# Forming two kinds of elementwise results on GpSimd instead of VectorE around the start of w_down

## The chip, the cores and the metric

The kernel runs on one core of a Trainium2 chip. The metric is device time in microseconds for one execution. Five engines matter: TensorE (PE in the profile, its weight loads PEld), VectorE (DVE), ScalarE (ACT), GpSimd (POOL) and SyncE (SP), which here issues the DMAs. Each engine takes its instructions in the order in which they stand in its queue; a row that waits holds up what stands behind it.

## The reference

One encoder layer: two attention mixers, an output projection, then a gated feed-forward network with a depthwise convolution, and a final RMSNorm. SEQ = D_MODEL = 1024, D_FF = 2816, all float32. The change lies in the feed-forward part:

```python
h2 = rmsnorm(x, g_ffn[i]) * (1 + scale2) + shift2
u = depthwise_conv_seq(h2 @ w_up[i], conv_w[i], conv_b[i])       # three taps along the sequence
u_val, u_gate = jnp.split(u, 2, axis=-1)
x = x + gate2 * ((jax.nn.gelu(u_gate, approximate=True) * u_val) @ w_down[i])
return rmsnorm(x, g_final)
```

## The kernel before, in words

Every float32 product is made of a high and a low half of each operand (`h`, `l` at a tile's name): three matmuls (lines L948, L949, L950) take high by high, high by low, low by high. On top of that w_up and w_down go by Strassen's scheme in Winograd's form, with seven block products in place of eight. `STEPS` names their operands: 11 x B11, S2 x T2, S1 x T1, S3 x T3, 12 x B21, S4 x B22, 22 x T4. S1 to S4 are sums and differences of a weight's four blocks; T1 to T4 of the other matrix's: T1 = B12 - B11, T2 = B22 - T1, T3 = T2 - B11, T4 = B21 - T2.

**w_up** runs in 22 jobs, t = 0 to 21, of 84 matmuls each. What `products` yields goes to `done` and `finish`: ScalarE adds the bias (L1138), VectorE the convolution's taps (L1144), ScalarE takes the gelu of the gate half (L1170), then the product of the two halves is formed (L1171, 128x1024), and SP stores it to DRAM, `a_scr` (L1172, `as<-big`).

**w_down** runs in 12 jobs, `jobs = (g0, q)`: three groups of three rows each (g0 = 0, 3, 6; `G` is 3), and four jobs of 63 matmuls to a group. A job's weights come in two loads (`down_load`, L1055, tiles `wraw`, of which there are two), and `a_operands` makes of them S1 (L912), S2 (L913), S3 (L914) on GpSimd and S4 on VectorE (L921). `split` makes the halves: high on ScalarE (L55), low on GpSimd (L56): `whi`/`wlo` of blocks 11 and 12, `wsh`/`wsl` of S2 with S1 and of S3 with 22, and a `big` tile for S4. The last reader of a raw tile lets SP load the next job's.

A group's operands come from `b_operands`, once for four jobs; I call the place where the next group's are made a transition. The first lies at the end of w_up and serves jobs 0 to 3, the second serves jobs 4 to 7, the third jobs 8 to 11. SP reads the stored rows (L1007), GpSimd forms T1 (L1018) and T2 (L1019) for the group's three rows. `moved` then copies a source to PSUM on ScalarE (`stage`, L998), takes the high half on ScalarE (L999) and the low half on VectorE (L1000). Its `then` is called with the copy in PSUM: for T2 it forms T3 in the place of B11 (L1028), for B21 it forms T4 (L1030). Behind the 12 jobs four rows are left over for an end phase.

A planner orders the instructions of each engine by a model of their times where the code does not set the order by hand; in `finish` the last job of w_up gets a lower priority (`offset=-300`).

Of the kernel before, what the change touches and what calls it, by code (L numbers as in the profile page):

```python
# [12 lines left out]
OP = mybir.AluOpType  # L13
# [6 lines left out]
FF = 22  # L20
# [8 lines left out]
def hybrid_encoder(tc, xT, c, w_ada, small, w_in, p1_bias, p23_bias, na_bias, ln2_mult, ident, w_br, w_out,  # L29
                   w_up, w_down, out):  # L30
    nc = tc.nc
    act, dve, pool, pe, sp = nc.scalar, nc.vector, nc.gpsimd, nc.tensor, nc.sync
# [897 lines left out]
    def products(st, n, moving, done, seq=range(7), in_psum=False):  # L930

        p, c = {}, {}

        def bank(x_):
            p[x_] = ps.tile([128, 512], FT, name="pj", bufs=6)
            return p[x_]

        def tmp(x_):
            c[x_] = wide()
            return c[x_]  # L940
        for j in seq:
            a, b = STEPS[j]
            x_ = "abcdacd"[j]
            psum = bank(x_) if j < 4 else p[x_]
            whi, wlo = st[a]
            for k in range(n):
                bhi, blo = moving(b, k)
                pe.matmul(psum, whi[:, k], bhi, start=j < 4 and k == 0, stop=False, skip_group_check=True)  # L948
                pe.matmul(psum, whi[:, k], blo, start=False, stop=False, skip_group_check=True)  # L949
                pe.matmul(psum, wlo[:, k], bhi, start=False, stop=k == n - 1, skip_group_check=True)  # L950
                if k == 1:
                    yield -1
            if j == 0:
                act.activation(tmp("t"), psum, AF.Copy)
            elif j == 1:
                dve.tensor_tensor(c["t"], psum, c["t"], OP.add)
            elif j == 2:
                dve.tensor_tensor(tmp("v"), psum, c["t"], OP.add)
            elif j == 3:
                dst = p["b"] if in_psum else c["v"]  # L960
                dve.tensor_tensor(dst, psum, c["v"], OP.add)  # L961
                done(1, 1, dst)
            elif j == 4:
                done(0, 0, psum)
            elif j == 5:
                dve.tensor_tensor(psum, psum, c["t"], OP.add)
                done(0, 1, psum)
            else:
                dst = psum if in_psum else c["t"]
                dve.tensor_tensor(dst, psum, c["t"], OP.add)  # L970
                done(1, 0, dst)
            yield j
# [8 lines left out]
    def wide(dtype=FT):  # L981
        return keep.tile([128, 512], dtype, name="wc", bufs=5)

    def big(shape, dtype=FT):
        return keep.tile(shape, dtype, name="big", bufs=9)
# [7 lines left out]
    def moved(n, src, then=None):  # L993

        hi, lo = ((work2 if n in ("B11", "T2", "T1", "T3") else work1[n]).tile(
            [128, 512], FR, name=n + e, bufs=G) for e in "hl")
        copy = ps.tile([128, 512], FT, name="stage", tag=next(stages))
        act.activation(copy, src, AF.Copy)  # L998
        act.activation(hi, src, AF.Copy)  # L999
        dve.tensor_tensor(lo, copy, f(hi), OP.subtract)  # L1000
        if then:
            then(copy)
        return hi, lo

    def a_load(i):
        ra = big([128, S])
        sp.dma_start(ra, a_scr[i])  # L1007
        return ra

    def b_operands(g0, mov):  # L1010

        ra = [[a_load(i + 11 * j) for j in range(2)] for i in range(g0, g0 + G)]
        b = [(r[0][:, :512], r[0][:, 512:], r[1][:, :512], r[1][:, 512:]) for r in ra]
        yield
        t1 = [wide() for _ in range(G)]
        for k in range(G):
            b11, t2, b21, b22 = b[k]
            pool.tensor_tensor(t1[k], t2, b11, OP.subtract)  # L1018
            pool.tensor_tensor(t2, b22, t1[k], OP.subtract)  # L1019
        yield  # L1020
        for n, src in (("B11", 0), ("T2", 1), ("T1", None), ("T3", 0), ("B21", 2), ("B22", 3), ("T4", 2)):
            mov[n] = []
            for k in range(G):
                b11, t2, b21, b22 = b[k]

                def then(copy):
                    if n == "T2":
                        dve.tensor_tensor(b11, copy, b11, OP.subtract)  # L1028
                    if n == "B21":
                        dve.tensor_tensor(b21, copy, t2, OP.subtract)  # L1030
                mov[n].append(moved(n, t1[k] if n == "T1" else b[k][src], then))
            yield
# [103 lines left out]
    with tc.tile_pool(name="up", bufs=2, reuse_waits="tile") as work:  # L1136
        def conv_in(y, t, hf, src):
            act.activation(y[:, halves[hf]], src, AF.Identity, bias=conv[:, 3, t:t + 1], scale=conv[:, 1, t:t + 1])  # L1138

        def conv_taps(y, t, ph):  # L1140
            w0, w2 = conv[:, 0, t:t + 1], conv[:, 2, t:t + 1]

            def tap(dst, src, wt):
                dve.scalar_tensor_tensor(y[:, dst], src, wt, y[:, dst], OP.mult, OP.add)  # L1144
            tap(slice(256, 768), ph[0], w0)
            tap(slice(768, 1024), ph[1][:, 0:256], w0)
            tap(slice(1, 256), ph[1][:, 256:511], w0)
            tap(slice(0, 256), ph[0][:, 256:512], w2)
            tap(slice(256, 768), ph[1], w2)
            tap(slice(768, 1023), ph[0][:, 1:256], w2)  # L1150

        def up_products(t, st, seq=range(7)):
            u, ys = [{}, {}], {i: big([128, S]) for i in range(2) if t == FF - 1}

            def done(i, hf, src):
                u[i][hf] = src
                if len(u[i]) == 1 and t < 2:
                    return
                with tc.high_priority(offset=-300 if t == FF - 1 else 0):
                    finish(i, hf)  # L1160

            def finish(i, hf):
                if i not in ys:
                    ys[i] = big([128, S])
                for n in range(2) if t < 2 else (hf,):
                    conv_in(ys[i], t + FF * i, n, u[i][n])
                if len(u[i]) == 2:
                    conv_taps(ys[i], t + FF * i, u[i])
                if len(u[0]) + len(u[1]) == 4:
                    act.activation(ys[1], ys[1], AF.Gelu_apprx_tanh)  # L1170
                    dve.tensor_tensor(ys[0], ys[0], ys[1], OP.mult)  # L1171
                    sp.dma_start(a_scr[t], ys[0])  # L1172
            return products(st, 4, lambda n, k: late[n][k] if n in late else (ops[n][0][:, k], ops[n][1][:, k]), done,
                            seq)
# [25 lines left out]
        t2 = big([128, 2, 512])  # L1200
        t2 = [t2[:, 0], t2[:, 1], wide(), wide()]
# [256 lines left out]
```

## Time and profile before

| what | before |
|---|---|
| median of 3 runs | 1569.3 us (1565.9 to 1570.37) |
| the profiled execution | 1566.2 us, span of its trace 1564.4 us |
| granted TensorE clock, mean | 0.982 |
| TensorE busy | 1509.5 us, 96% of the span |
| VectorE busy | 1024.4 us, 65% |
| ScalarE busy | 805.8 us, 52% |
| GpSimd busy | 801.8 us, 51% |

The span runs from the first to the last instruction of the trace. In the timelines each row has its start, its duration (us), engine, line, operation, `out<-in`, shape and count, and in brackets how long the engine sat idle before it and what ended that. The chain of work that ended last is followed back from the last instruction. The w_up jobs end at about 1324 us of the span, the jobs of w_down lie from there to about 1500 us.

### The profile page before, as it was taken

Reading aid. Unit: us, or ns where it says so; the run is one execution under the profiler, and the core shown is the slowest. Engines: PE = TensorE matmul, PEld = TensorE weight load, DVE = VectorE, ACT = ScalarE, POOL = GpSimd, SP = SyncE. Lnnn points to the kernel's source line nnn. Section 1 sums busy time; section 2 is a strip of 40 time slices with the busy share of each in tenths; the row PEclk is TensorE's granted clock in tenths of the full one; section 3 lists DMA queues with packets and bytes.
Section 4 is the critical chain, followed back from the end, with each engine's and each line's share of the span. In section 5 each row is a group of like instructions: output and inputs, shape, how many; then the busy total and the mean of one; then the engine's idle time right before and its main releaser. Section 6 shows DMA issues by size and latency. Waiting matters only on the chain. (4 is left out here: it accounts for less than half of the span.)

```text
span 1564.4 us, 22094 instructions
## 1 busy us (share of the span) xinstructions
PE 1509.5 (96%) x8012; PEld 1291.5 (83%) x8012; DVE 1024.4 (65%) x1874; ACT 805.8 (52%) x1448; POOL 801.8 (51%) x500
## 2 busy tenths in 40 slices
PE   8999799999999999999999888999999999999998
PEld 7899788888887998888888767888888887788787
DVE  6686266676756665535625888766666667877775
ACT  4432366666766677643335454444444446575542
POOL 1242243444337566411256858666666665679621
PEclk9899899999999999999999999999999999999999
DMA  9458522223133453557734212322222223533313
GB/s 352 164 201 292 156 73 73 81 77 93 51 90 111 141 138 104 184 187 238 228 128 149 74 54 81 108 81 81 81 82 90 86 74 136 182 114 121 115 54 109
DMA packets 114421, 196.87 MB, mean 126 GB/s; under 512 B 40200, under 2 KB 61576, under 8 KB 114312
## 3 DMA queue, kind: packets, MB, share of 16 engines
q1 hardware_dynamic: 114040, 195.20, 38.0%
q8 instruction: 63, 1.03, 0.3%
q14 instruction: 46, 0.38, 0.1%
q10 hardware_dynamic: 272, 0.26, 0.1%
HBM read 158.73 MB, written 42.47 MB: 129 GB/s over the span
## 5 line engine op out<-in xcount | busy, mean ns | idle before, releaser
L56 POOL TENSOR_TENSOR wlo<-wraw,whi 128x1024 fp32r<-128x1024 f32 (+2 forms) x78 | 179.9, 2307 | 284.1 <-ACT whi L55 275.1
L79 PE MATMUL pj<-h,whi 128*128 128x512 f32 x448 | 180.5, 403 | 3.8 <-ACT h L202 2.2
L80 PE MATMUL pj<-h,whi 128*128 128x512 f32 x448 | 179.4, 400 | 0.3 <-DVE h L204 0.3
L81 PE MATMUL pj<-h,wlo 128*128 128x512 f32 x448 | 178.8, 399 | 0.0
L56 POOL TENSOR_TENSOR wsl<-big,wsh 128x1024 fp32r<-128x1024 f32 (+1 forms) x45 | 109.3, 2432 | 50.6 <-ACT wsh L55 50.6
L1144 DVE SCALAR_TENSOR_TENSOR big<-wc,sm,big 128x256 f32<-128x256 f32 (+1 forms) x132 | 115.0, 919 | 17.3 <-ACT big L1138 17.2
L55 ACT ACTIVATE whi<-wraw 128x1024 fp32r<-128x1024 f32 (+2 forms) x81 | 81.3, 1003 | 87.0 <-PE pj L80 25.9
L338 POOL TENSOR_SCALAR kl<-kl 64x512 fp32r<-64x512 f32 x32 | 63.8, 1994 | 80.4 <-DVE kl L336 78.1
L79 PEld LDWEIGHTS pj<-h,whi 128*128 128x128 f32 x448 | 85.3, 190 | 20.6 <-ACT ks L337 3.4
L80 PEld LDWEIGHTS pj<-h,whi 128*128 128x128 f32 x448 | 85.4, 191 | 15.9 <-DVE h L204 1.1
L81 PEld LDWEIGHTS pj<-h,wlo 128*128 128x128 f32 x448 | 85.2, 190 | 15.0
L575 DVE CUSTOM_DVE_ANT_0 P<-S,bias 128x256 f32<-128x256 f32 x128 | 52.3, 420 | 53.7 <-PE S L622 31.9
L576 ACT ACTIVATE P<-P,st 128x256 f32<-128x256 f32 x128 | 64.3, 503 | 39.3 <-DVE st L575 38.7
L1144 DVE SCALAR_TENSOR_TENSOR big<-pj,sm,big 128x512 f32<-128x512 f32 x132 | 67.9, 564 | 16.1 <-ACT big L1138 16.1
L56 POOL TENSOR_TENSOR wsl<-wraw,wsh 128x768 fp32r<-128x768 f32 (+1 forms) x23 | 50.1, 2178 | 47.7 <-ACT wsh L55 47.7
L1138 ACT ACTIVATE big<-wc,sm 128x512 f32<-128x512 f32 x44 | 35.8, 816 | 74.5 <-DVE wc L961 45.6
L239 PE MATMUL pv<-vwh,h 128*128 128x256 f32 x256 | 73.7, 288 | 0.4 <-ACT vs L246 0.4
L240 PE MATMUL pv<-vwl,h 128*128 128x256 f32 x256 | 72.5, 283 | 0.0
L241 PE MATMUL pv<-vwh,h 128*128 128x256 f32 x256 | 72.5, 283 | 0.0
L527 POOL TENSOR_TENSOR vv<-vv 96x256 fp32r<-96x256 f32 (+2 forms) x32 | 41.0, 1294 | 59.3 <-ACT vv L526 59.1
L55 ACT ACTIVATE wsh<-big 128x1024 fp32r<-128x1024 f32 (+1 forms) x45 | 44.9, 1002 | 35.4 <-POOL big L913 18.3
L1170 ACT ACTIVATE big<-big 128x1024 f32<-128x1024 f32 x22 | 23.3, 1060 | 76.6 <-DVE big L1144 76.6
(379 smaller groups left out, 4923.7 us busy)
## 6 DMA issues: line engine op xcount, KB each, us to landing
wraw<-w_in SPq DMA_DIRECT2D x36, 512.0 KB, 3.5
wada<-w_ada SPq DMA_DIRECT2D x31, 512.0 KB, 7.1
big<-w_up SPq DMA_DIRECT2D x22, 512.0 KB, 5.0
wraw<-w_up SPq DMA_DIRECT2D x22, 512.0 KB, 3.7
as<-big SPq DMA_DIRECT2D x22, 512.0 KB, 3.0
big<-as SPq DMA_DIRECT2D x22, 512.0 KB, 8.1
wraw<-w_down SPq DMA_DIRECT2D x24, 384.0 KB, 4.2
gs<-gs SPq DMA_DIRECT2D x32, 256.0 KB, 2.5
```

The source lines that it names most:

```text
L55: act.activation(hi, raw, AF.Copy)
L56: lo_eng.tensor_tensor(lo, raw, f(hi), OP.subtract)
L79: pe.matmul(psum, whi[:, k0 + k], mhi, start=k == 0, stop=False)
L80: pe.matmul(psum, whi[:, k0 + k], mlo, start=False, stop=False)
L81: pe.matmul(psum, wlo[:, k0 + k], mhi, start=False, stop=k == n - 1)
L239: pe.matmul(p, hhi, hi[:, k], start=fresh and k == 0, stop=False, skip_group_check=True)
L240: pe.matmul(p, hhi, lo[:, k], start=False, stop=False, skip_group_check=True)
L241: pe.matmul(p, hlo, hi[:, k], start=False, stop=k == KT - 1, skip_group_check=True)
L338: pool.tensor_scalar(ll[b], f(ll[a]), 1.0, None, OP.mult)
L575: dve.tensor_tensor_reduce(pp, d, bias, -1.0, BIG, OP.add, OP.min, mi)
L576: act.activation(pp, pp, AF.Exp, bias=mi, scale=-1.0, accum_out=li)
L1144: dve.scalar_tensor_tensor(y[:, dst], src, wt, y[:, dst], OP.mult, OP.add)
```

## The change

T3 = T2 - B11 of w_down's operands is formed on GpSimd from `t2`, the tile in SBUF, where VectorE formed it from the copy in PSUM: three instructions of 128x512 at each of the three transitions, nine in all. And the product of gelu and value is formed on GpSimd, not on VectorE, for t >= FF - 2, which is t = 20 and t = 21, so two of 22 jobs.

```diff
@@ in b_operands
                 def then(copy):
                     if n == "T2":
-                        dve.tensor_tensor(b11, copy, b11, OP.subtract)
+                        pool.tensor_tensor(b11, t2, b11, OP.subtract)
@@ in up_products, finish
                     act.activation(ys[1], ys[1], AF.Gelu_apprx_tanh)
-                    dve.tensor_tensor(ys[0], ys[0], ys[1], OP.mult)
+                    (dve if t < FF - 2 else pool).tensor_tensor(ys[0], ys[0], ys[1], OP.mult)
                     sp.dma_start(a_scr[t], ys[0])
```

The planner orders the queues anew with it. Up to w_up's last jobs all rows stand as they did. GpSimd's queue at the first transition, before (from the last low half of w_up's weights on; L1018 and L1019 are T1 and T2 of the first group, L912 to L914 and L56 belong to w_down's job 0, the last two rows to job 1):

```order
L56 TENSOR_TENSOR wsl<-big,wsl 128x512
L1018 TENSOR_TENSOR wc<-big 128x512 x3
L1019 TENSOR_TENSOR big<-big,wc 128x512 x3
L912 TENSOR_TENSOR big<-wraw 128x384
L913 TENSOR_TENSOR big<-big,wraw 128x384
L914 TENSOR_TENSOR wraw<-wraw 128x384
L56 TENSOR_TENSOR wsl<-big,wsh 128x768
L56 TENSOR_TENSOR wsl<-wraw,wsh 128x768
L56 TENSOR_TENSOR big<-wraw,big 128x384
L56 TENSOR_TENSOR wlo<-wraw,whi 128x2x384
L912 TENSOR_TENSOR big<-wraw 128x384
```

The same place now (the first L1171 is the product of t = 20, the second that of t = 21):

```order
L56 TENSOR_TENSOR wsl<-big,wsl 128x512
L1171 TENSOR_TENSOR big<-big 128x1024
L1018 TENSOR_TENSOR wc<-big 128x512 x3
L1019 TENSOR_TENSOR big<-big,wc 128x512 x3
L912 TENSOR_TENSOR big<-wraw 128x384
L1028 TENSOR_TENSOR big<-big 128x512 x3
L913 TENSOR_TENSOR big<-big,wraw 128x384
L914 TENSOR_TENSOR wraw<-wraw 128x384
L56 TENSOR_TENSOR wsl<-big,wsh 128x768
L56 TENSOR_TENSOR wsl<-wraw,wsh 128x768
L1171 TENSOR_TENSOR big<-big 128x1024
L56 TENSOR_TENSOR big<-wraw,big 128x384
```

Behind these follow `wlo<-wraw,whi` and L912 of job 1, as before. So one product stands ahead of the operands, the three T3 stand between S1 and S2 of job 0, and the other product stands ahead of job 0's last read of a raw tile.

On SP, where the two loads of job 1 (L1055) and the store of t = 21 (L1172) stand among loads of x (L801), the difference is this:

```order
 L801 DMA x_12221<-xs 128x512
-L1055 DMA wraw<-w_down 128x2x384 x2
+L1055 DMA wraw<-w_down 128x2x384
+L1172 DMA as<-big 128x1024
+L1055 DMA wraw<-w_down 128x2x384
 L801 DMA x_12322<-xs 128x512
 L801 DMA x_12324<-xs 128x512
 L801 DMA x_12326<-xs 128x512
 L801 DMA x_12328<-xs 128x512
-L1172 DMA as<-big 128x1024
```

The store stands now between the two loads.

GpSimd's queue at the third transition, before (operands of the last group, among the weights of jobs 8 and 9):

```order
L1018 TENSOR_TENSOR wc<-big 128x512 x2
L56 TENSOR_TENSOR wsl<-wraw,wsh 128x768
L1019 TENSOR_TENSOR big<-big,wc 128x512
L1018 TENSOR_TENSOR wc<-big 128x512
L1019 TENSOR_TENSOR big<-big,wc 128x512
L56 TENSOR_TENSOR wlo<-wraw,whi 128x2x384
L912 TENSOR_TENSOR big<-wraw 128x384
L1019 TENSOR_TENSOR big<-big,wc 128x512
L913 TENSOR_TENSOR big<-big,wraw 128x384
```

And now:

```order
L1018 TENSOR_TENSOR wc<-big 128x512
L56 TENSOR_TENSOR wsl<-big,wsh 128x768
L1028 TENSOR_TENSOR big<-big 128x512
L56 TENSOR_TENSOR big<-wraw,big 128x384
L1019 TENSOR_TENSOR big<-big,wc 128x512
L1018 TENSOR_TENSOR wc<-big 128x512
L56 TENSOR_TENSOR wsl<-wraw,wsh 128x768
L1028 TENSOR_TENSOR big<-big 128x512
L1019 TENSOR_TENSOR big<-big,wc 128x512
L56 TENSOR_TENSOR wlo<-wraw,whi 128x2x384
L912 TENSOR_TENSOR big<-wraw 128x384
L1028 TENSOR_TENSOR big<-big 128x512
```

L913 and L914 follow. The three T3 stand among the splits of the neighbouring jobs.

## The prediction

> **What bounds the kernel now.** I read the page first, then TensorE's waits in the region that the change touches, then the chain of work that ended last, then the timelines of GpSimd, ScalarE and VectorE there.
>
> ```profile
> PE 1509.5 (96%) x8012; PEld 1291.5 (83%) x8012; DVE 1024.4 (65%) x1874; ACT 805.8 (52%) x1448; POOL 801.8 (51%) x500
> ```
>
> TensorE is busy 96% of 1564.4 us, so over the whole span it bounds; VectorE at 65% and GpSimd at 51% look free. That share is a mean over many stages, and says nothing on the stage of this change, which begins at about 1304 us (the rows of all queues stand in the same order until then). TensorE's waits from 1290 to 1520 us are only three:
>
> ```profile
> PE pj L949 <- DVE T1l L1000: 2.7, 1, 2.7
> PE pj L949 <- DVE T2l L1000: 1.7, 1, 1.7
> PE pj L950 <- POOL wlo L56: 0.7, 1, 0.7
> ```
>
> Two are on VectorE (2.7 + 1.7 = 4.4 us), at the step from w_up to w_down; they are what the change can take away. The third is on GpSimd, inside w_down. The chain that ended last tells how near GpSimd is to being the bound of w_down:
>
> ```profile
> 1387.11 1.86 POOL wsl L56
> 1388.97 0.99 POOL big L56
> 1389.97 4.24 DMA wraw<-w_down
> 1394.38 0.99 POOL big L912
> ...
> 1447.49 4.06 DMA wraw<-w_down
> ...
> 1502.20 0.69 DVE wc L958
> 1502.94 0.50 PE pj L948
> ```
>
> From 1387.11 to 1502.94 no matmul stands in this chain. It is a loop: GpSimd splits a job's weights (L56), its last read of the raw tile lets the next load start, the load lands 4.1 to 4.4 us later, GpSimd forms the differences (L912 to L914), splits, and so on. The busy times of three stretches of w_down say the same (the columns after the length are TensorE, its weight loads, VectorE, ScalarE, GpSimd, then the granted clock):
>
> ```profile
> 1331.60:1338.40 6.80, 5.76 (x14) 4.39 (x15) 6.80 (x11) 4.19 (x7) 3.10 (x3) 0.50 0.68 247
> 1337.06:1394.35 57.29, 57.29 (x250) 47.04 (x248) 45.30 (x69) 36.47 (x63) 44.18 (x33) 0.99 0.46 157
> 1394.35:1451.68 57.33, 57.20 (x251) 46.76 (x250) 44.64 (x66) 35.04 (x61) 46.08 (x34) 1.00 0.33 110
> ```
>
> Four jobs of GpSimd last 57.29 us, four of TensorE (4 x 63 matmuls, 57.29 / 252 = 0.227 us from one to the next, with nothing between) as much. GpSimd is busy 44.18 us of it; the rest is mostly its wait for the weights' DMA, which its own work starts. So the loop of GpSimd and DMA and TensorE run level. Where they touch shows in these rows:
>
> ```profile
> 1329.01 1.02 POOL L56 TENSOR_TENSOR big<-wraw,big 128x384 fp32r<-128x384 f32 x1 [1.36 <-ACT big L55]
> 1334.06 1.84 POOL L56 TENSOR_TENSOR wlo<-wraw,whi 128x768 fp32r<-128x768 f32 x1 [4.04 <-ACT whi L55]
> 1337.06 1.01 POOL L912 TENSOR_TENSOR big<-wraw 128x384 f32<-128x384 f32 x1 [1.16 <-DVE big L1171]
> 1394.35 1.02 POOL L912 TENSOR_TENSOR big<-wraw 128x384 f32<-128x384 f32 x1 [4.40 <-DMA wraw<-w_down]
> 1395.33 1.85 POOL L56 TENSOR_TENSOR wlo<-wraw,whi 128x768 fp32r<-128x768 f32 x1
> 1454.74 1.83 POOL L56 TENSOR_TENSOR wlo<-wraw,whi 128x768 fp32r<-128x768 f32 x1
> 1397.34 0.40 PE L950 MATMUL pj<-B11h,wlo 128*128 128x512 f32 x1
> 1456.62 0.51 PE L950 MATMUL pj<-B11h,wlo 128*128 128x512 f32 x1 [0.68 <-POOL wlo L56]
> ```
>
> The low half of the fifth weights is ready at 1395.33 + 1.85 = 1397.18 and read at 1397.34: slack 0.16 us. That of the ninth is ready at 1456.57 and already waited for, by 0.68. Whatever makes this loop later at those two places, TensorE pays.
>
> **The change, part by part.** *Prices.* Off VectorE go nine differences and two products; onto GpSimd come the same, and GpSimd's durations for equal shapes stand in the trace (its own 128x512 differences of L1018; a 128x1024 subtraction of L56 for the product):
>
> ```profile
> L1028 DVE TENSOR_TENSOR big<-stage,big x9: 674/681/682, 1321.3 to 1443.2; 128x512 f32<-128x512 f32 x9
> 1292.69 1.23 DVE L1171 TENSOR_TENSOR big<-big 128x1024 f32<-128x1024 f32 x1 [0.59 <-ACT big L1170]
> 1305.67 1.29 POOL L1018 TENSOR_TENSOR wc<-big 128x512 f32<-128x512 f32 x1
> 1293.77 2.41 POOL L56 TENSOR_TENSOR wsl<-big,wsh 128x1024 fp32r<-128x1024 f32 x1 [4.67 <-ACT wsh L55]
> ```
>
> So three differences cost GpSimd 3 x 1.29 = 3.9 us at each of three transitions, and a product 2.41. VectorE is spared 9 x 0.68 + 2 x 1.23 = 8.6 us; it is not in the chain between 1387 and 1502.20, so I count that at nothing there. The covers are TensorE's matmuls and the loop itself; only the 4.4 us of waits on T2l and T1l could come back, and those lie ahead of the first place where the loop binds.
>
> *The first transition.* The product of w_up's last but one job now stands on GpSimd ahead of the three L1018, and the three L1028 stand ahead of L913. These were:
>
> ```profile
> 1309.45 1.06 ACT L1170 ACTIVATE big<-big 128x1024 f32<-128x1024 f32 x1 [2.40 <-DVE big L1144]
> 1317.85 1.02 POOL L913 TENSOR_TENSOR big<-big,wraw 128x384 f32<-128x384 f32 x1
> 1322.60 0.84 ACT L55 ACTIVATE wsh<-big 128x768 fp32r<-128x768 f32 x1
> 1324.66 0.39 PE L948 MATMUL pj<-T2h,wsh 128*128 128x512 f32 x1
> ```
>
> GpSimd waits for the gelu (ends 1310.5), then 2.41 of product, 3.9 of L1018, 3.9 of L1019, 1.0 of L912, 3.9 of L1028: L913 starts at about 1325.6 where it was 1317.85. ScalarE's split of S2 (wsh) moves from 1322.60 to 1326.6 or later, and TensorE's first T2 product from 1324.66 to 1327.5 or later. TensorE so gets a new wait of about 2.8 us, and keeps some of the old 4.4: VectorE has three L1028, 2.0 us, less ahead of T1l. I put the net on TensorE between -4.4 and +3, near nothing; it does not decide, because of the next point.
>
> *The last product ahead of the weights' release.* GpSimd's rows now have the product of w_up's last job ahead of L56 `big<-wraw`, the last read of job 0's raw tile. The gelu it waits for:
>
> ```profile
> 1333.88 1.04 ACT L1170 ACTIVATE big<-big 128x1024 f32<-128x1024 f32 x1
> ```
>
> ends at 1334.92. Then 2.41 (product) + 1.02 (L56 `big<-wraw`) + 4.41 (load, from the 1389.94 at which that L56 ended to L912 at 1394.35) = 1342.76 for L912 of job 1, which was at 1337.06: the loop starts 5.7 us late. If the gelu comes 2 us earlier, since VectorE's taps have less ahead, it is 3.7; if 1.3 later, 7.0. On SP the store of that product stands now between the two loads of job 1; it waits for the product that GpSimd does ahead of `big<-wraw` anyway, so it holds the second load by nothing more than its own issue.
>
> *From there to the first touch.* +3.9 for L1028 at the second transition. Against it stand GpSimd's short waits for ScalarE between the two places, in which a later loop can catch up:
>
> ```profile
> 1341.17 1.86 POOL L56 TENSOR_TENSOR wsl<-big,wsh 128x768 fp32r<-128x768 f32 x1 [1.04 <-ACT wsh L55]
> 1358.13 1.85 POOL L56 TENSOR_TENSOR wsl<-wraw,wsh 128x768 fp32r<-128x768 f32 x1 [0.70 <-ACT wsh L55]
> 1384.82 1.86 POOL L56 TENSOR_TENSOR wsl<-big,wsh 128x768 fp32r<-128x768 f32 x1 [0.54 <-ACT wsh L55]
> 1387.11 1.86 POOL L56 TENSOR_TENSOR wsl<-wraw,wsh 128x768 fp32r<-128x768 f32 x1 [0.43 <-ACT wsh L55]
> ```
>
> 2.7 us at most. The waits for the DMA (4.4) give nothing back, since the load starts only when GpSimd is done. So the fifth weights are 5.7 + 3.9 - 2.7 = 6.9 late, and TensorE waits 6.9 - 0.16 = 6.7 there or in jobs 1 to 4 ahead of it.
>
> *Third transition.* +3.9 again, with no slack (the 0.68 wait): TensorE waits 3.9 more. Sum: 6.7 + 3.9 = **+10.6 us**.
>
> *What has no row.* A TensorE wait also costs clock: behind the two waits of before, the stretch 1331.6 to 1338.4 was granted 0.50:
>
> ```profile
> 1333.65 0.63 PE L948 MATMUL pj<-T1h,wsh 128*128 128x512 f32 x1
> 1337.92 0.63 PE L948 MATMUL pj<-B11h,whi 128*128 128x512 f32 x1
> ```
>
> Ten matmuls further, 4.27 us: 0.43 apart instead of 0.23, so 14 of them lost 2.8 us. New waits may bring one or two such stretches (0 to 5.6); since the loop, not TensorE, sets the time behind them, I take 0. Behind 1502.94 TensorE goes on to the end of the program, with no work moved there; I bound a new order around it by the length of the link ahead, 0.69, either way, and take 0.
>
> **What the lock does.** VectorE's ops with both inputs in SBUF are stretched while GpSimd works, those with one in PSUM are not:
>
> ```profile
> 1297.10 0.48 DVE L1144 SCALAR_TENSOR_TENSOR big<-wc,sm,big 128x256 f32<-128x256 f32 x1 [0.88 <-ACT big L1138]
> 1323.53 2.12 DVE L1144 SCALAR_TENSOR_TENSOR big<-wc,sm,big 128x255 f32<-128x255 f32 x1
> ```
>
> The tap at 1323.53 took 2.12 instead of 0.48, until GpSimd's op of 1323.52 ended; L1028, whose copy lies in PSUM, never took more than 0.682. On GpSimd, L1028 reads both operands from SBUF, so each can hold up a tap by its 1.29 us: up to 3.9 us later for the gelu at 1333.88 and so for the last product. The Trainium skill ("SBUF — State Buffer", section "Who interferes with whom") states this as an exclusive lock: of a VectorE op with two SBUF inputs and a GpSimd op that reads SBUF, whoever comes first keeps the shared pair for its whole instruction, and a VectorE op with one SBUF input stays free of it. The rows above agree with it; by that rule the moved operation turns from one that collides with nobody into one that does, and the sum would be +14.5 instead of +10.6. I keep +10.6, because L913 at 1325.6 puts the three L1028 at 1321.7 to 1325.6, so that only the tap of 1323.53 and its next neighbours can meet them, and what reads PSUM did not collide.
>
> **The rivals.**
> - *Partly absorbed* (+2 to +7): the gelu comes 2 us early and GpSimd fits its new work into the DMA waits, since the second load of a job starts with the other tile's last read. For it: the loop of a plain job is shorter than TensorE's 57.29 / 4 = 14.32, as 1337.06 to the next L912 shows:
>
> ```profile
> 1349.56 1.02 POOL L912 TENSOR_TENSOR big<-wraw 128x384 f32<-128x384 f32 x1 [3.74 <-DMA wraw<-w_down]
> ```
>
> 12.5 us. Against it: the touch at 1397.34 with 0.16 slack shows that the surplus of jobs 1 to 4 is already spent by the job with the transition.
> - *Nothing measurable* (within 2 us): the two VectorE waits vanish with their half clock, and the loop gives back as much.
> - *Faster*: VectorE at the first transition is the bound, and the loop is in the chain only because it runs level with TensorE. TensorE then loses both waits, 1.7 + 2.7, and the 2.8 us of half clock at 1331.6 to 1338.4: -7.2, so 1569.3 - 7.2 = 1562.1. It decides at the ninth weights: by the sum the loop has them 5.7 + 3.9 - 2.7 + 3.9 = 10.8 us late there, and it would have to have them 7.2 early, so a new order of its rows would have to save it 18 us, about one job. For it: the gelu and the product, for which L912 waited at 1337.06, come after VectorE's taps. Against it: L913, which ran 6.8 us ahead of its use at 1324.66, now stands behind 7.8 us of other work, and nothing of the loop's work is taken away. I give it more than the rows alone would, since the order of GpSimd's and ScalarE's rows in w_down is new nearly everywhere and I read its worth least surely.
> - *The lock* (above): +14 to +18, 1583 to 1587.
>
> **How the numbers follow.** The profiled execution took 1566.2 us (span 1564.4), the median of the runs is 1569.3, 3.1 above it. On the profiled one the sum gives 1576.8, on the median 1579.9. Chances: loop late by 7 to 14 us 0.58; the lock besides 0.07; partly absorbed 0.13; nothing 0.08; faster 0.14. About 0.3% of 1569.3, 4.7 us, is what a measurement tells from no change; of the partly absorbed case 0.08 lie below that. So slower 0.70, same 0.16, faster 0.14. The likeliest case alone spans 1576 to 1583; the range goes down to 1565 (0.3% below the median, so that of the faster case nearly all is left out) and up to 1586.
>
> **What would show it.** Right: in the new trace TensorE's waits name GpSimd (wlo, wsl) or ScalarE's wsh behind it, some 6 us before 1400 and about 4 more around 1460; L912 of job 1 starts near 1343; T2 and T1 waits on VectorE shrink; GpSimd is busy near 818 us (801.8 + 9 x 1.29 + 2 x 2.41). Wrong: L912 of job 1 at about 1337 in spite of the product ahead, or the fifth `wlo` ready several us before its matmul; then the loop had slack that I have read away. A new wait of over 4 us at T2 would show the first transition to be mis-sized.

## The result: 0.55% slower, and the profile after

The changed kernel takes 1577.21 us (median of 6 runs, 1575.78 to 1581.26) against 1569.49 us of the kernel before (6 runs, 1565.9 to 1573.73): the ratio is 1.0055, 95% interval [1.0039, 1.007], so +7.7 us. The profiled execution has a span of 1574.0 us where it was 1564.4.

The page's first row, and the engines' shares of the chain that ended last (in before GpSimd had 4% and the DMA 2% of it):

```profile
PE 1513.1 (96%) x8012; PEld 1295.0 (82%) x8012; DVE 1018.0 (65%) x1863; ACT 805.4 (51%) x1448; POOL 816.8 (52%) x511
PE 35%; DVE 5%; ACT 2%; issue 1%; POOL 1%; DMA 0%; DVEq 0%; ACTq 0%
```

GpSimd is busy 15.0 us more (16.4 had been worked out), VectorE 6.4 us less, and no share says that this is slower. TensorE's waits from 1290 to 1530 us do:

```profile
PE pj L948 <- ACT wsh L55: 7.5, 3, 4.1
PE pj L949 <- DVE T1l L1000: 3.5, 1, 3.5
PE pj L950 <- POOL wlo L56: 1.2, 1, 1.2
PE pj L950 <- POOL wsl L56: 0.3, 1, 0.3
```

12.5 us, where it was 5.1. The largest row is new: TensorE waits for `wsh`, the high half of S2, which ScalarE makes. GpSimd and ScalarE at the first transition:

```profile
1311.13 2.40 POOL L1171 TENSOR_TENSOR big<-big 128x1024 f32<-128x1024 f32 x1 [4.14 <-ACT big L1170]
1322.17 3.82 POOL L1028 TENSOR_TENSOR big<-big 128x512 f32<-128x512 f32 x3
1325.94 1.19 POOL L913 TENSOR_TENSOR big<-big,wraw 128x384 f32<-128x384 f32 x1
1330.18 2.37 POOL L56 TENSOR_TENSOR wsl<-big,wsh 128x768 fp32r<-128x768 f32 x1 [2.11 <-ACT wsh L55]
1337.35 2.39 POOL L1171 TENSOR_TENSOR big<-big 128x1024 f32<-128x1024 f32 x1 [2.85 <-ACT big L1170]
1344.54 1.02 POOL L912 TENSOR_TENSOR big<-wraw 128x384 f32<-128x384 f32 x1 [1.71 <-DMA wraw<-w_down]
```

```profile
1328.74 0.63 ACT L999 ACTIVATE T3h<-big 128x512 fp32r<-128x512 f32 x1
1329.26 0.84 ACT L55 ACTIVATE wsh<-big 128x768 fp32r<-128x768 f32 x1
```

```profile
1330.16 0.79 PE L948 MATMUL pj<-T2h,wsh 128*128 128x512 f32 x1 [4.06 <-ACT wsh L55]
1335.71 0.80 PE L949 MATMUL pj<-T1l,wsh 128*128 128x512 f32 x1 [3.48 <-DVE T1l L1000]
1396.88 0.50 PE L948 MATMUL pj<-T2h,wsh 128*128 128x512 f32 x1 [2.58 <-ACT wsh L55]
1454.06 0.50 PE L950 MATMUL pj<-B11h,wlo 128*128 128x512 f32 x1 [1.21 <-POOL wlo L56]
1459.03 0.50 PE L948 MATMUL pj<-T2h,wsh 128*128 128x512 f32 x1 [0.81 <-ACT wsh L55]
```

S2's difference (L913) starts at 1325.94 where it was 1317.85, and ends at 1327.1. ScalarE splits it only at 1329.26, since its queue now has moves of T3, B22 and stage copies ahead. The wait is 4.06 us. All three high halves of T3 stand ahead of `wsh` in that queue, where before they came behind it.

To place the loss, I take the start of TensorE's n-th matmul (counted from 0), less that of the n-th in before, and subtract this difference at the 6800th matmul (1297.16 us in before, ahead of the change: 1.28 us in the changed kernel). All traces have 8012 matmul records. Each column holds the loss up to its place:

| kernel | time ratio, 95% interval | behind the 1st transition (7080th, 1369 us) | behind the 2nd (7300th, 1420 us) | behind all of w_down's jobs (7720th, 1517 us) |
|---|---|---|---|---|
| the change | 1.0055 [1.0039, 1.007] | +2.4 | +6.5 | +8.3 |
| T3 alone | 1.0067 [1.0046, 1.0089] | +2.3 | +4.5 | +7.6 |
| both products alone | 1.003 [1.0015, 1.0045] | +1.9 | +2.6 | +4.7 |
| T3 and product of t = 20 | 1.0078 [1.0056, 1.0101] | +3.2 | +5.3 | +8.9 |
| product of t = 21 alone | 1.002 [1.0005, 1.0034] | -0.1 | +2.6 | +3.2 |
| T3 of groups 2 and 3 | 1.002 [1.0004, 1.0036] | -0.5 | +1.4 | +3.7 |
| T3 of group 1 | 1.0023 [1.0009, 1.0038] | +1.8 | +5.9 | +6.8 |
| the change, T3 behind S2 | 1.0076 [1.0064, 1.0088] | +0.9 | +7.0 | +10.2 |
| T3 alone, behind S2 | 1.0035 [1.0022, 1.0047] | -1.8 | -0.4 | +6.0 |
| T3 of group 1, behind S2 | 0.9984 [0.9971, 0.9996] | -1.8 | -2.0 | -2.9 |
| the change, S3 on VectorE | 1.0096 [1.0072, 1.0119] | +2.8 | +13.2 | +16.7 |
| before, S3 on VectorE | 1.0031 [1.0021, 1.0042] | -0.6 | +1.3 | +1.7 |
| T3 on VectorE, from SBUF | 1.0027 [1.0012, 1.0041] | -2.5 | +1.3 | +5.1 |

The columns are of one profiled execution each; the ratios are of 5 to 32 runs, and the two differ by up to some 3 us (T3 of group 1: +6.8 in its profile, 0.23% or 3.6 us in its runs). Several ratios lie at 0.2 to 0.3%, where I had put the edge of what a measurement tells from no change: their intervals leave out 1, but by little.

### The profile page after: what moved, and what is told of

Read it like the earlier page. It is cut to its first block, busy times and chain, and to the rows that moved or that the text cites. A ratio compares the mean times of both kernels' runs of the same rounds, so it can differ in the third digit from the quotient of the medians.

```text
span 1574.0 us, 22099 instructions
## 1 busy us (share of the span) xinstructions
PE 1513.1 (96%) x8012; PEld 1295.0 (82%) x8012; DVE 1018.0 (65%) x1863; ACT 805.4 (51%) x1448; POOL 816.8 (52%) x511
## 5 line engine op out<-in xcount | busy, mean ns | idle before, releaser
L56 POOL TENSOR_TENSOR wlo<-wraw,whi 128x1024 fp32r<-128x1024 f32 (+2 forms) x78 | 179.8, 2306 | 296.5 <-ACT whi L55 265.7
L56 POOL TENSOR_TENSOR wsl<-big,wsh 128x1024 fp32r<-128x1024 f32 (+1 forms) x45 | 110.2, 2450 | 50.8 <-ACT wsh L55 50.8
L56 POOL TENSOR_TENSOR wsl<-wraw,wsh 128x768 fp32r<-128x768 f32 (+1 forms) x23 | 49.9, 2169 | 46.1 <-ACT wsh L55 46.1
```

What stands on the lines that cost most here:

```text
L56: lo_eng.tensor_tensor(lo, raw, f(hi), OP.subtract)
```

## The experiments

**The parts.** Which part costs, and at which transition?

```diff
 T3 alone:                      L1171 on dve for all t
 both products alone:           L1028 on dve, from copy
 T3 and product of t = 20:      (pool if t == FF - 2 else dve)
 T3 of groups 2 and 3:          L1028 on pool only if g0 > 0; L1171 on dve
```

> T3 of all three groups is formed on GpSimd, both products stay on VectorE. Loop theory (the one of the prediction: GpSimd's added microseconds make the loop of splits and loads late): no lateness from the product, 3.9 - 2.7 - 0.16 = 1.0 at the second transition and 3.9 at the third, +4.9 us over before. Queue theory (formed on the trace of after: what costs is what stands ahead of S2's difference L913 on GpSimd and of its split wsh on ScalarE when TensorE reaches the T2 product): the first transition about 0, since without the product L913 comes at about 1322 and its split in time for 1324.7; the second 4.1 and the third 2.0 as in the changed kernel, +6 us, and TensorE's waits there name ScalarE's wsh.

> Both products (t = 20 and 21) on GpSimd, T3 stays on VectorE. Loop theory: 5.7 - 2.7 - 0.16 = +2.8 us, taken at the fifth weights, nothing at the third transition. Queue theory: L913 of job 0 stands behind one product only and comes at about 1322, so the first transition costs 0 to 1; the second product, ahead of the release of a raw tile, costs nothing that TensorE sees: 0 to +1 us in all.

> The change without the product of t = 21, which stays on VectorE. Loop theory: the 5.7 us of lateness go, +4.9 us remain over before. Queue theory: the product of t = 21 never mattered, +8 us as with the whole change, with waits of 4 us on wsh at the first transition and 2.6 at the second.

> T3 on GpSimd for the second and third group only; the first group's T3 and both products stay on VectorE. Loop theory: +4.9 us (1.0 + 3.9). Queue theory: 4.1 + 2.0 = +6 us, the first transition as before (waits of 1.7 and 2.7 us on T2l and T1l).

T3 alone costs as much as the whole change. So the queue theory's zero at the first transition was wrong: without the product TensorE waits nearly as long there. GpSimd's L913 comes when that theory had it (1326.63, and this trace is 5.12 us behind before's, so 1321.5), but ScalarE's split of it starts only 4.95 us behind its end. In between ScalarE works without a gap, at the high halves of all three T3 and B22 among other rows:

```profile
1326.63 1.01 POOL L913 TENSOR_TENSOR big<-big,wraw 128x384 f32<-128x384 f32 x1
1332.59 0.83 ACT L55 ACTIVATE wsh<-big 128x768 fp32r<-128x768 f32 x1
```

```profile
1333.47 0.79 PE L948 MATMUL pj<-T2h,wsh 128*128 128x512 f32 x1 [3.53 <-ACT wsh L55]
1339.13 0.80 PE L949 MATMUL pj<-T1l,wsh 128*128 128x512 f32 x1 [3.58 <-DVE T1l L1000]
```

So GpSimd's delay of S2 is only a part of it: T3, formed early, brings its moves ahead of `wsh` in ScalarE's queue.

The two products alone cost 0.30%, 4.7 us, in three small pieces: more than either theory had (+2.8, and 0 to +1). T3 of groups 2 and 3 costs 0.20%, 3.1 us (+3.7 in the column), less than either (+4.9 and +6). With T3 and only the product of t = 20, GpSimd's L912 of job 1 stands here (this trace runs 1.30 us ahead of before's, so 1341.94 on before's scale, where it was 1337.06):

```profile
1340.64 1.02 POOL L912 TENSOR_TENSOR big<-wraw 128x384 f32<-128x384 f32 x1 [0.17 <-DMA wraw<-w_down]
```

It is 4.9 us late without the product that the prediction held to be the cause, against 6.2 with it (1344.54 - 1.28 = 1343.26). And the kernel is no faster for it. That decides for the queue theory on this term.

**One part at a time.**

```diff
 T3 of group 1:                 L1028 on pool only if g0 == 0; L1171 on dve
 product of t = 21 alone:       (pool if t == FF - 1 else dve); L1028 on dve
```

> T3 on GpSimd for the first group only, later groups and both products as before. Queue theory (a difference ahead of S2 delays ScalarE's split wsh, and GpSimd's lateness of 4.6 us at job 1 runs on to the next transition): +2.4 at the first transition as in T3 alone, and something of 0 to 3 at the second, where the late loop meets an otherwise unchanged order: +2.5 to +6 us. If only the loop's added work counted (3.9 us, then 53 us with 2.7 us of waits to make it up): +1.

> Only the product of t = 21 on GpSimd. Loop theory: it is the 5.7 us of the prediction, +2.8 us at the fifth weights. Queue theory: it stands behind all of job 0's S2, and where the planner puts it here (behind the last read of the raw tile) it delays no load: 0 to +1 us, and L912 of job 1 at 1337 to 1339.

T3 of the first group costs at the first transition (+1.8) and again at the second, where nothing was moved: GpSimd's loop is still late, and TensorE waits for the split of the fifth weights.

```profile
1408.47 0.64 PE L950 MATMUL pj<-B11h,wlo 128*128 128x512 f32 x1 [1.86 <-POOL wlo L56]
```

So lateness of the loop, 4.8 us at L912 of job 5 (1405.62, less 6.47, against 1394.35), does last from one transition to the next, as the prediction had it; only its source was another. The product of t = 21 by itself moves L912 of job 1 by little:

```profile
1334.76 2.38 POOL L1171 TENSOR_TENSOR big<-big 128x1024 f32<-128x1024 f32 x1
1337.22 1.03 POOL L912 TENSOR_TENSOR big<-wraw 128x384 f32<-128x384 f32 x1
```

This trace runs 1.10 us ahead, so L912 is 1.3 us late. It costs 0.2% by the times, near the loop theory's +2.8 us and above the queue theory's 0 to 1, though not for the reason given: here it stands behind the tile's release.

**The order alone.** The same instructions on GpSimd, but each T3 held behind S2 (its call moves from T2's step of the loop to T3's own):

```diff
+        behind[:] = [pool.tensor_tensor(S2, S1, a11, OP.subtract)]        # L913
...
+                if n == "T3":
+                    with tc.issue_after(behind[0].ins):
+                        pool.tensor_tensor(b11, t2, b11, OP.subtract)     # L1028
 T3 of group 1, behind S2:      the same only if g0 == 0, else on dve as before
```

> T3 of all groups on GpSimd but held behind S2; both products on VectorE. The same instructions as T3 alone, which was +0.67%, in another order. Loop theory: no better than T3 alone, +5 to +10 us. Queue theory: nearly all of it goes, -2 to +2 us over before, since the first transition has L913 where it was and VectorE has 2 us less ahead of T1l.

> The changed kernel with all its work on GpSimd, but each T3 is held behind the S2 difference of the next job on GpSimd's queue, so ScalarE's split wsh also comes ahead of T3's moves. Loop theory (GpSimd's added microseconds count, wherever they stand): as the changed kernel, +8 to +10 us over before. Queue theory (what stands ahead of S2 counts): TensorE's waits on wsh at the three transitions go; the first transition costs about 2 as with the products alone, the second and third under 1 each: +2 to +5 us.

> The same three differences of the first group on GpSimd, but held behind S2 of job 0; later groups' T3 on VectorE as before. Queue theory: the first transition gains 1.8 us as in the run with all groups held (VectorE's waits on T2l and T1l shrink), the second and third are as before unless the planner sets them anew: -2 to 0 us, and it is the only version so far that could be faster. Loop theory: +1, as with the first group ahead of S2.

At the first transition the place decides: T3 ahead of S2 loses 2.3 us, behind S2 it gains 1.8. The place on GpSimd's queue brings that on ScalarE's with it: `wsh` comes ahead of all moves of T3 again. With only the first group moved so, the kernel is the one version that is not slower than before: 0.9984 [0.9971, 0.9996], 1.4 us less in the medians (1567.49 against 1568.93), which is below the 0.3% that I had called measurable and beside an interval that only just leaves out no change. GpSimd's T3 stands in the time in which it waited for ScalarE, and TensorE's waits of 4.4 us in VectorE's name go down to 2.9:

```profile
1322.36 4.13 POOL L1028 TENSOR_TENSOR big<-big 128x512 f32<-128x512 f32 x3
1326.59 1.89 POOL L56 TENSOR_TENSOR wsl<-big,wsh 128x768 fp32r<-128x768 f32 x1
```

```profile
PE pj L950 <- DVE T1l L1001: 2.9, 2, 2.6
```

At the other two transitions holding T3 back fails, and the queue theory with it: 0.76% and 0.35%, 11.9 and 5.5 us, are near what the loop theory had (+8 to +10, +5 to +10). But the waits name something that neither theory has. With both products, TensorE's longest wait at the second transition is for T3's high half:

```profile
1391.57 8.61 DVE L922 TENSOR_TENSOR wraw<-wraw,big 128x384 f32<-128x384 f32 x1
1400.22 0.52 ACT L55 ACTIVATE big<-wraw 128x384 fp32r<-128x384 f32 x1 [4.87 <-DVE wraw L922]
1400.65 0.61 ACT L1000 ACTIVATE T3h<-big 128x512 fp32r<-128x512 f32 x1
1401.31 0.79 PE L949 MATMUL pj<-T3h,wsh 128*128 128x512 f32 x1 [4.31 <-ACT T3h L1000]
```

GpSimd had formed all three T3 by 1396.22. ScalarE moves them late because the split of S4 stands ahead in its queue, and that waits 4.87 us for S4's difference on VectorE (L922), which takes 8.61 us.

Without the products it loses 6.4 us between the second column and the third, mostly in VectorE's name, and it is the same row. VectorE's rows there, GpSimd's, and TensorE's (L915 is S3, L1049 the accumulation L1047):

```profile
1445.30 8.51 DVE L922 TENSOR_TENSOR wraw<-wraw,big 128x384 f32<-128x384 f32 x1
1454.34 1.39 DVE L1049 SCALAR_TENSOR_TENSOR x<-pj,ada,x 128x512 f32<-128x512 f32 x2
```

```profile
1445.09 1.01 POOL L915 TENSOR_TENSOR wraw<-wraw 128x384 f32<-128x384 f32 x1
1446.08 3.79 POOL L1028 TENSOR_TENSOR big<-big 128x512 f32<-128x512 f32 x3
...
1451.60 1.79 POOL L56 TENSOR_TENSOR wsl<-wraw,wsh 128x768 fp32r<-128x768 f32 x1
1454.45 1.00 POOL L56 TENSOR_TENSOR big<-wraw,big 128x384 fp32r<-128x384 f32 x1 [1.05 <-ACT big L55]
```

```profile
1455.13 0.80 PE L949 MATMUL pj<-T1h,wsh 128*128 128x512 f32 x1 [4.58 <-DVE x L1049]
```

S4's difference has both inputs in SBUF. It takes 0.55 us where GpSimd rests, and here 8.51: six GpSimd instructions (the first of 1445.09) follow each other without a gap until 1453.39, and it ends 0.4 us behind. VectorE's accumulation, which frees the bank that TensorE wants, stands behind it.

**Less work on GpSimd.**

```diff
-        pool.tensor_tensor(a21, a11, a21, OP.subtract)
+        (dve if n == G else pool).tensor_tensor(a21, a11, a21, OP.subtract)
```

> The changed kernel, with S3 of w_down's twelve jobs formed on VectorE instead of GpSimd (12 x 1.02 us less on GpSimd, ahead of the release of the raw tiles). Loop theory: the loop is 4 us shorter per four jobs, which takes back the second and third transition: about +2 to +3 us over before. Queue theory: T3 stands ahead of S2 at the first transition as before, so +2.4 stays there, and ScalarE's wsh behind the moves at the second and third: +5 to +8 us.

> The kernel before, with only S3 of w_down's jobs on VectorE instead of GpSimd. Both theories: TensorE waits only 0.7 us on GpSimd in before, so -1 to +1 us; the wait at the ninth weights goes if the loop is what makes it.

With 12 us taken off GpSimd, the change becomes slower still, +0.96%, the largest ratio of all. The loop theory had it faster than the change, the queue theory at most as slow; both were wrong. In the kernel before, the same edit costs 0.31%, 4.9 us, where both had -1 to +1. S3 on VectorE has two SBUF inputs and falls into the same trap, at the second transition:

```profile
1388.68 6.77 DVE L914 TENSOR_TENSOR wraw<-wraw 128x384 f32<-128x384 f32 x1 [1.94 <-POOL big L912]
1395.98 0.68 DVE L961 TENSOR_TENSOR pj<-pj,wc 128x512 f32<-128x512 f32 x1
```

```profile
1388.57 1.32 POOL L1019 TENSOR_TENSOR big<-big,wc 128x512 f32<-128x512 f32 x1
...
1393.74 1.30 POOL L1028 TENSOR_TENSOR big<-big 128x512 f32<-128x512 f32 x1
```

```profile
1396.71 0.80 PE L948 MATMUL pj<-T4h,wsh 128*128 128x512 f32 x1 [7.20 <-DVE pj L961]
```

GpSimd's run of five without a gap ends at 1395.04, VectorE's instruction at 1395.45. Most of TensorE's wait of 7.20 us follows from it: without a hold L914 would have been done some 6.2 us earlier (6.77 less the 0.56 that it takes elsewhere in this trace).

**No work moved.**

```diff
-                        dve.tensor_tensor(b11, copy, b11, OP.subtract)
+                        dve.tensor_tensor(b11, t2, b11, OP.subtract)
```

> Nothing changes engine: T3 stays on VectorE, but reads T2 from SBUF instead of the copy in PSUM, so that the planner orders ScalarE, VectorE and TensorE anew from the first transition on. If the planner's new order by itself costs (order theory): +2 to +8 us with no work moved, and waits at the second and third transition. If the work on GpSimd costs: within 1 us of before. A collision of the two SBUF inputs with GpSimd would show as T3 longer than 0.68 us, at most 9 x 1.3 us on VectorE.

+0.27%, 4.3 us, with nothing moved off or onto GpSimd. TensorE gains 2.5 us at the first transition and loses 3.8 at each of the second and the third, among them this wait:

```profile
1466.12 0.80 PE L948 MATMUL pj<-T2h,wsh 128*128 128x512 f32 x1 [3.22 <-ACT wsh L55]
```

T3 now has two SBUF inputs, and its durations (min, median, max, in ns) show it beside the 674/681/682 of before:

```profile
L1028 DVE TENSOR_TENSOR big<-big x9: 681/1183/2098, 1322.0 to 1449.6; 128x512 f32<-128x512 f32 x9
```

So the run doesn't part the new order from the collisions: nine instructions are some 4.5 us longer by the median, on an engine with room. It shows that a loss of half the change's size needs no work on GpSimd.

## Why the prediction was right

The time (1577.2, forecast 1579.9) and the sign came out, and two of the named signs did: waits on `wsh`, and L912 of job 1 near 1343. That the size came so near is in part luck, since errors of both signs make it up, as the steps show:

- *The first transition, "near nothing".* Failed: +2.4 us, and the sign that the prediction had given for it, a new wait of over 4 us at T2, came. L913 came where it was put (1325.94, less 1.28 is 1324.7, forecast 1325.6), but ScalarE's split came 2.1 us behind L913's end, since its queue was ordered anew, and the wait was 4.06 where 2.8 was worked out. T1l's wait did not shrink either (3.48, was 2.73): ScalarE's copy of T1 waited for VectorE's T2l, which stood behind two taps that took 2.69 us while GpSimd split `wsl` (1330.18 above), and T1l itself stood behind a third tap, of 1.69:

```profile
1330.14 2.69 DVE L1144 SCALAR_TENSOR_TENSOR big<-wc,sm,big 128x512 f32<-128x512 f32 x2
1332.76 0.68 DVE L1000 TENSOR_TENSOR T2l<-stage,T2h 128x512 fp32r<-128x512 f32 x1
```

```profile
1333.47 0.60 ACT L998 ACTIVATE stage<-wc 128x512 f32<-128x512 f32 x1 [2.15 <-DVE T2l L1000]
```

- *L912 of job 1, 5.7 us late.* It was 6.2 late, and by the chain that was forecast: the gelu (1.1 later than before), the product, the last read, a load of 3.8. But that product is not what costs: without it L912 is still 4.9 late, since ScalarE's split of S4, at 1328.42 before, then comes at 1335.89 on before's scale, behind the late T1 and the gelu. T3 alone makes 4.6 (1346.73, less 5.12, is 1341.61), and the product of t = 21 adds 1.3.
- *+3.9 for T3 at the second transition.* At job 4's S1 GpSimd is 5.1 us late (one T3 stands ahead of it, and of the 2.7 us of short waits most was given back), at its S2 9.3:

```profile
1392.86 1.01 POOL L913 TENSOR_TENSOR big<-big,wraw 128x384 f32<-128x384 f32 x1
```

(1382.27 in before, plus 1.28). In between stand two T3 and, in the new order, `wlo`, 4.4 us. So the lateness was there, and larger than the 6.9 forecast.
- *"TensorE waits 6.7".* It lost 4.1 (6.5 - 2.4), and not on `wlo` at the place with 0.16 of slack, but on `wsh`, which ScalarE started 2.1 us behind L913's end, with moves of B22, T3 and a stage copy ahead:

```profile
1394.94 0.63 ACT L999 ACTIVATE B22h<-big 128x512 fp32r<-128x512 f32 x1
...
1395.98 0.84 ACT L55 ACTIVATE wsh<-big 128x768 fp32r<-128x768 f32 x1
```

In the new order of rows `wlo` comes ahead of L912, so the row with 0.16 of slack was no longer the tight one. The wait itself is 2.58; most of the other 1.5 us is clock, the term that the prediction had taken at 0 because the loop was to set the time. Behind the wait the granted clock (last but two of the columns) was 0.62, and 1.00 at this place in before:

```profile
1396.88:1401.43 4.55, 4.55 (x12) 3.27 (x13) 3.38 (x6) 3.72 (x8) 4.53 (x3) 0.62 0.02 5
```

- *+3.9 at the third.* It was 1.8 (8.3 - 6.5).
- *The lock.* The priced form (a tap held up by one T3 at 1.29 us) did not show: the tap in that time took 0.98 us. But the three taps ahead of T1l were held up by GpSimd's splits at the first transition (above), and in the runs with T3 behind S2 or S3 on VectorE a hold was far longer than 1.29 us (below).

So the sum 0 + 6.7 + 3.9 = 10.6 stood against 2.4 + 4.1 + 1.8 = 8.3: the first term was missing, the other two were too large. The theory behind it, that GpSimd's microseconds count wherever they stand, fell: the same T3 at another place in the queue gains at the first transition, and fewer microseconds on GpSimd made it slower. What stays open is why each order the planner made costs what it does at the second and third transition; e.g. T3 alone loses 2.2 us at the second, and the change 4.1. The parts don't add up either (0.67% and 0.30% against 0.55%). No run moves the work while the other queues keep their order, so how much of those two losses is the new order and how much the work is not shown.

## What to carry to other kernels

An engine with 50% of idle time is not free at the place where its queue meets the critical one: ask for each moved instruction what stands behind it there, and who waits for that, through the next engine's queue too. A planner that orders by its own model sets all queues anew for a small edit, so hold the one order that matters by hand and move only the part that falls into a real gap, here the first group's T3 behind S2. And look at each VectorE instruction with two SBUF inputs that others wait for, where GpSimd works without a gap: mostly it loses the rest of one GpSimd instruction, but now and then the whole stretch. T3 with one input in PSUM never took more than 0.68 us.

## What the runs showed of the hardware

A VectorE instruction with two SBUF inputs is held up by GpSimd, mostly for the rest of one instruction. Four rows of before show it, S4's difference of job 1 and of job 2 with GpSimd's two rows at the latter:

```profile
1340.49 0.55 DVE L921 TENSOR_TENSOR wraw<-wraw,big 128x384 f32<-128x384 f32 x1
1353.40 1.35 DVE L921 TENSOR_TENSOR wraw<-wraw,big 128x384 f32<-128x384 f32 x1 [0.81 <-POOL big L913]
1353.31 1.03 POOL L914 TENSOR_TENSOR wraw<-wraw 128x384 f32<-128x384 f32 x1
1354.33 2.15 POOL L56 TENSOR_TENSOR wsl<-big,wsh 128x768 fp32r<-128x768 f32 x1
```

The second took 1.35 us where 0.55 is its time alone: it ended 0.41 us behind the end of GpSimd's L914. GpSimd's next row starts there without a gap, but takes 2.15 us instead of 1.85, so VectorE had its turn between the two. In some cases it had not: 6.77, 8.51 and 8.61 us, where GpSimd had five and six in a row, and each ended 0.4 us behind the first gap in GpSimd's queue. These are rare. In the 14 traces, 118 differences of S3, S4 and T3 on VectorE with two SBUF inputs started while GpSimd was in an instruction that the next followed within 0.1 us (from 1300 to 1530 us of the span). 111 of them ended 0.4 to 0.6 us behind the end of that one; three were passed by two instructions, one by three (3.85 us), and three by five or six. What decides who gets the turn is not shown. The Trainium skill ("SBUF — State Buffer", section "Who interferes with whom") says that the one that comes first keeps the pair for its whole instruction; the traces agree that the other is fully blocked, and show that now and then it stays blocked for several instructions that follow each other at once.

The last stage's clock differs from one profiled execution to another. The stretch from 1538 to 1544.8 us of the two products alone was granted half the clock (the last but two of the columns), though TensorE has no idle time in it; before was granted 1.00 from 1530 to 1550 us:

```profile
1538.00:1544.80 6.80, 6.80 (x33) 6.80 (x34) 1.20 (x4) 1.04 (x3) 0.73 (x1) 0.50 0.01 4
```

Four of the 14 profiled executions have such a stretch at the same matmuls (the 7800th to the 7840th), of some 3.4 or 6.8 us, worth 1.5 or 3 us; what brings it about wasn't tried. That is why the losses are counted up to 1517 us.
